# Tables of powers times B and powers times C made on GpSimd one batch ahead, in buffers of their own

## The chip, the cores and the metric

The kernel runs on one core of a Trainium2 chip. The metric is the time of one execution on the device, in microseconds (us). The core has five engines that run side by side, each with its own queue of instructions that it executes in order: TensorE (PE, matrix products), VectorE (DVE), ScalarE (ACT), GpSimd (POOL) and SyncE (SP), which here issues most of the DMAs. An instruction waits for semaphores of the others, and whatever is queued behind it on its engine waits too.

## The reference, cut to what matters

One layer of an encoder over 1024 tokens of width 1024: a norm, a wide product z = hn @ w_in, four mixers on slices of z (a gated recurrence, a neighbourhood attention, a state space mixer, a pooling), and a gated merge. The change concerns the state space mixer, which is for 32 groups of 16 channels, 64 complex states and two directions:

```python
for d in range(2):
    ...
    bu_r = jnp.einsum('bsgc,gpc->bsgp', ug, bbar_r)
    bu_i = jnp.einsum('bsgc,gpc->bsgp', ug, bbar_i)
    _, _, sr, si = lax.associative_scan(_complex_combine, (a_r, a_i, bu_r, bu_i), axis=1, reverse=(d == 1))
    yd = (jnp.einsum('bsgp,gcp->bsgc', sr, c_re[d]) - jnp.einsum('bsgp,gcp->bsgc', si, c_im[d]))
    y = y + yd.reshape(bsz, s, w)
yg = jax.nn.gelu(y)
return yg * jax.nn.sigmoid(yg @ glu_w + glu_b)
```

## The kernel before, in words

Every large product is made of three products of split operands (a high and a low part, `wh` and `wl`, `hnH` and `hnL`; lines 94 to 96, `mm3`). The program runs through stages: the norm, the attention, the state space mixer, its gated unit (`glu`), the recurrence (`lru`), the pooling, the merge. Products of z that no stage needs at once are the filler. They come from a generator, `z_gen`: each of its steps is 24 products of 128x512 into PSUM (`ps_z`, `ps_t`), with an eviction (ACT, and for the branch gates one DVE product, `bgt`), and every second step also splits a block of weights into `wh` (ACT) and `wl` (DVE).

`drive` mixes a stage with the filler. The stage is a generator that yields pairs (estimated PE time, estimated DVE time); a scale multiplies the DVE part, 1.25 for the state space stage, 1.35 for the gated unit and 0.95 for the recurrence. As long as the summed PE time is behind the DVE time, one filler step (5.2 of PE) is emitted:

```python
pe = dve = 0.0
for p, v in main:
    pe, dve = pe + p, dve + v * scale
    while filler is not None and pe < dve:
        c = next(filler, None)
        ...
        pe, dve = pe + c[0], dve + c[1]
```

What the filler has left after the recurrence is emitted then. A scheduler of the framework afterwards sets each engine's order from this order of emission and from its own simulated times. The queues of the order below are what it made.

The state space stage (`s5`) first makes parameters (`s5_params`): powers of the state matrix (`Ag`, `Aq`, `Pm`) and the inputs `Bb` and `Ct`. It then works through four batches (`s5_batch`) of 8 groups. In a batch, `Gf` is the table of powers times B (two tiles of 128x1024) and `Q` that of powers times C (two of 128x1280), each made of three elementwise operations with a temporary (`gt`, `qt`). PE transposes Gf into `Gt` (line 99) and multiplies Bb with Q (line 975), from which the short convolution `M` comes by way of DRAM. `E` holds further powers, made on DVE, and lies in the buffers of Gf. Then two halves follow: PE makes V from U and Gt (line 1022), DVE turns V into `vr` and `vi`, scans them (lines 1046 and 1048) and turns the results `xs` into `Xr` and `Xi`; PE adds U times M (line 1068), Xr times Q and Xi times Q (line 1070); ACT copies the sum to `Y`. Eight DMAs write Y of a batch to `ydr` in DRAM (line 1075). The gated unit reads it back as `gy` (line 1085), makes the gelu (`gt`, `yg`, split into `ygH` and `ygL`), and multiplies with the split weights `gw`.

Of the kernel before, what the change touches and what calls it, by code (L numbers as in the profile page):

```python
# [9 lines left out]
F32 = mybir.dt.float32  # L10
# [3 lines left out]
ALU = mybir.AluOpType  # L14
# [17 lines left out]
class Kern:  # L32
# [23 lines left out]
    def tt(self, out, a, b, op):  # L56
        self.nc.vector.tensor_tensor(out, a, b, op)
# [847 lines left out]
    def s5(self):  # L905
        self.ydr = self.dp.tile([W, 8, 128], F32, name="ydr")
        self.kd = [self.dp.tile([16, 2, 4, 240], F32, name=f"kd{k}") for k in range(4)]
        with self.tc.tile_pool(name="sp", bufs=1, reuse_waits="tile") as sp:
            with self.tc.tile_pool(name="sq", bufs=1, reuse_waits="tile") as sq:
                self.s5_params(sp, sq)  # L910
            yield 1.0, 22.0
            with self.tc.tile_pool(name="sb", bufs=1, reuse_waits="tile") as sb:
                for ct in range(4):
                    yield from self.s5_batch(sb, ct)

    def s5_batch(self, sb, ct):
        nc = self.nc
        g8 = slice(ct * 8, ct * 8 + 8)

        def bcg(tab, n):  # L920
            return tab[:, :, g8].rearrange("p n g -> p g n").unsqueeze(3).broadcast_to([128, 8, n, 16])

        def bcc(m, n):
            return m.unsqueeze(2).broadcast_to([128, 8, n, 16])
        Bv = [bcc(b[:, g8, 0:16], 8) for b in self.Bb]
        Cv = [bcc(c.rearrange("p (g c) -> p g c", c=16)[:, g8, :], 10) for c in self.Ct]

        U = sb.tile([128, 8, 128], F32, tag="U", name="U")
        for t in range(8):
# [1 line left out]
                              self.ud[ct * 128:ct * 128 + 128, t, :].rearrange("(g c) j -> c g j", c=16))  # L931

        Gt = []
        gs = [128, 8, 8, 16]
        Gf = [sb.tile(gs, F32, tag=f"Gf{k}", name=f"Gf{k}") for k in range(2)]
        gt = sb.tile(gs, F32, tag="tmpA", name="gt")
        self.mul(Gf[0], bcg(self.Ag[0], 8), Bv[0])
        self.mul(gt, bcg(self.Ag[1], 8), Bv[1])
        self.sub(Gf[0], Gf[0], gt)
        gt = sb.tile(gs, F32, tag="tmpA", name="gt")  # L940
        self.mul(Gf[1], bcg(self.Ag[0], 8), Bv[1])
        self.mul(gt, bcg(self.Ag[1], 8), Bv[0])
        self.add(Gf[1], Gf[1], gt)
        yield 0.0, 7.0
        for k in range(2):
            o = sb.tile([128, 8, 128], F32, tag=f"Gt{k}", name=f"Gt{k}")
            for h in range(2):
# [4 lines left out]
                self.copy_a(o[:, h * 4:h * 4 + 4, :], pt.rearrange("p (g n) -> p g n", g=4))  # L952
            Gt.append(o)
        yield 2.0, 0.0

        qs = [128, 8, 10, 16]
        Q = [sb.tile(qs, F32, tag=f"Q{k}", name=f"Q{k}") for k in range(2)]
        qt = sb.tile(qs, F32, tag="tmpA", name="qt")
        self.mul(Q[0], bcg(self.Aq[0], 10), Cv[0])
        self.mul(qt, bcg(self.Aq[1], 10), Cv[1])  # L960
        self.sub(Q[0], Q[0], qt)
        qt = sb.tile(qs, F32, tag="tmpA", name="qt")
        self.mul(Q[1], bcg(self.Aq[2], 10), Cv[0])
        self.mul(qt, bcg(self.Aq[0], 10), Cv[1])
        self.sub(Q[1], Q[1], qt)
        yield 0.0, 8.4

        pk = [self.ps("s").rearrange("p (a b) -> p a b", a=4) for _ in range(2)]
        for gi in range(2):
            for q in range(4):  # L970
                g = gi * 4 + q
                for half, lo in ((0, 0), (1, 2)):
                    p = slice(64 * half, 64 * half + 64)
                    for k in range(2):
                        nc.tensor.matmul(
                            pk[half][32 * q:32 * q + 32, gi, :],
                            self.Bb[k][p, ct * 8 + g, :],
                            Q[k][p, g, lo:lo + 8, :].rearrange("p t c -> p (t c)"),
                            start=(k == 0), stop=(k == 1),
# [21 lines left out]
        for m in range(7):  # L1001
            n = 1 << m
            b = [128, 8, n]
# [12 lines left out]
        for h in range(2):  # L1016
# [10 lines left out]
            vr, vi, t = (sb.tile(hv, F32, tag=n, name=n) for n in ("vr", "vi", "vt"))  # L1027
# [3 lines left out]
            t = sb.tile(hv, F32, tag="vt", name="vt")  # L1031
# [11 lines left out]
            for k, vv in ((0, vr), (1, vi)):  # L1043
                x = sb.tile(hv, F32, tag=f"xs{k}", name=f"xs{k}")
# [10 lines left out]
            t = sb.tile(hv, F32, tag="vt", name="vt")  # L1055
# [3 lines left out]
            t = sb.tile(hv, F32, tag="vt", name="vt")  # L1059
# [5 lines left out]
            for g in range(4):  # L1065
                c = slice(g * 128, g * 128 + 128)
                a = h * 4 + g
                nc.tensor.matmul(py[:, c], M[:, a, :], U[:, a, :], start=True, stop=False)
                for k in range(2):
                    nc.tensor.matmul(py[:, c], Q[k][:, a, 1:9, :].rearrange("p t c -> p (t c)"), X[k][:, c],  # L1070
                                     start=False, stop=(k == 1))
# [338 lines left out]
```

## Time and profile before

| | |
|---|---|
| median of 3 runs | 1368.45 us (1367.85 to 1368.73) |
| profiled execution | 1368.02 us, its span 1366.2 us |
| PE busy | 1346.5 us (99%) |
| DVE busy | 918.9 us (67%) |
| ACT busy | 565.0 us (41%) |
| POOL busy | 20.9 us (2%) |

The profile is of one execution. The span is the time from its first to its last recorded instruction. Busy time is the time in which an engine executes; the rest of the span it waits. In a row, a group of instructions is named by its line in the program, its engine, its operation and its tiles as out<-in. The state space stage's batches lie between about 408 and 702 us of the span.

### The profile page before, as it was taken

What the parts mean: (1) busy time and instruction counts of PE and PEld (TensorE: products, weight loads), DVE (VectorE), ACT (ScalarE), POOL (GpSimd) and SP (SyncE); (2) the same over time, 40 slices, a digit from 0 to 9 for tenths busy, and PEclk for the clock granted to TensorE, in tenths of its full rate; (3) what the DMA queues carried; (4) which work ended last, traced back from release to release, by engine and by line L of the source; (5) the groups of instructions that cost most, each with busy time, mean ns of one, the idle gap of its engine ahead of it and who ended that gap; (6) DMA issues with size and microseconds to landing.
All of it is one profiled execution on the core that took longest, in us unless ns stands there. A gap on an engine that the chain in (4) does not pass through costs nothing.

```text
span 1366.2 us, 19163 instructions
## 1 busy us (share of the span) xinstructions
PE 1346.5 (99%) x7354; PEld 1142.2 (84%) x7354; DVE 918.9 (67%) x1664; ACT 565.0 (41%) x881; POOL 20.9 (2%) x81
## 2 busy tenths in 40 slices
PE   7999999999999999999999999999999999999997
PEld 6999998888888888788888888888888888888885
DVE  6551676455289797979758367356465676896886
ACT  6552676587532221212134545526322211154552
POOL 2200000000000000000000000000000000000000
PEclk9999999999999999999999999999999999999998
DMA  9452134433344233323344142232824657433326
GB/s 326 130 146 65 54 83 121 131 97 121 86 120 120 81 100 121 94 96 103 118 160 162 57 153 97 82 139 89 298 99 175 240 170 268 164 108 124 124 93 216
DMA packets 141054, 181.98 MB, mean 133 GB/s; under 512 B 29200, under 2 KB 100888, under 8 KB 140962
## 3 DMA queue, kind: packets, MB, share of 16 engines
q1 hardware_dynamic: 140610, 180.72, 40.6%
q8 instruction: 58, 0.95, 0.3%
q14 instruction: 34, 0.28, 0.1%
q0 software_dynamic: 352, 0.03, 0.0%
HBM read 127.05 MB, written 54.03 MB: 133 GB/s over the span
## 4 chain that ended last, share of the span: by engine, by line
PE 92%; DVE 5%; DMA 1%; issue 1%; ACT 0%; SPq 0%; DVEq 0%
PE ps_z L94 15%; PE ps_z L95 15%; PE ps_z L96 15%; PE ps_t L96 4%; PE ps_t L95 4%; PE ps_t L94 4%; PE ps_t L99 3%; PE ps_o L94 3%; PE ps_o L96 3%; PE ps_o L95 3%; PE ps_s L94 3%; PE ps_s L96 3%; PE ps_s L95 3%; PE ps_o L580 2%; PE ps_s L545 2%; PE ps_z L1326 1%
## 5 line engine op out<-in xcount | busy, mean ns | idle before, releaser
L94 PE MATMUL ps_z<-hnH,wh 128*128 128x512 f32 x744 | 293.2, 394 | 2.0 <-DVE bgt L60 2.0
L95 PE MATMUL ps_z<-hnL,wh 128*128 128x512 f32 x744 | 292.0, 392 | 0.0
L96 PE MATMUL ps_z<-hnH,wl 128*128 128x512 f32 x744 | 291.8, 392 | 0.0
L94 PEld LDWEIGHTS ps_z<-hnH,wh 128*128 128x128 f32 x744 | 139.8, 188 | 30.8 <-DVE bgt L60 2.4
L96 PEld LDWEIGHTS ps_z<-hnH,wl 128*128 128x128 f32 x744 | 139.8, 188 | 28.5 <-issue 0.4
L95 PEld LDWEIGHTS ps_z<-hnL,wh 128*128 128x128 f32 x744 | 139.8, 188 | 27.8 <-issue 0.4
L66 DVE TENSOR_TENSOR wl<-wr,wh 128x1024 fp32r<-128x1024 f32 x72 | 88.0, 1222 | 101.2 <-ACT wh L82 101.1
L82 ACT ACTIVATE wh<-wr 128x1024 fp32r<-128x1024 f32 x72 | 76.1, 1059 | 148.6 <-PE ps_z L95 81.1
L94 PE MATMUL ps_z<-wh,hnH 128*128 128x256 f32 x384 | 108.3, 285 | 0.5 <-ACT zqk L82 0.5
L96 PE MATMUL ps_z<-wh,hnL 128*128 128x256 f32 x384 | 108.5, 287 | 0.0
L95 PE MATMUL ps_z<-wl,hnH 128*128 128x256 f32 x384 | 108.1, 283 | 0.0
L95 PE MATMUL ps_t<-hnL,wh 128*128 128x512 f32 x216 | 84.2, 390 | 0.0
L94 PE MATMUL ps_t<-hnH,wh 128*128 128x512 f32 x216 | 84.1, 389 | 0.0
L96 PE MATMUL ps_t<-hnH,wl 128*128 128x512 f32 x216 | 84.0, 389 | 0.0
L94 PEld LDWEIGHTS ps_z<-wh,hnH 128*128 128x128 f32 x384 | 73.2, 191 | 1.2 <-ACT zqk L82 1.2
L95 PEld LDWEIGHTS ps_z<-wl,hnH 128*128 128x128 f32 x384 | 73.5, 192 | 0.0
L96 PEld LDWEIGHTS ps_z<-wh,hnL 128*128 128x128 f32 x384 | 72.9, 192 | 0.0
L551 DVE CUSTOM_DVE_ANT_0 sc<-ps_s,bias 128x384 f32<-128x384 f32 x64 | 34.2, 555 | 27.2 <-PE ps_s L545 14.6
L94 PE MATMUL ps_o<-my,wh 128*128 128x512 f32 x128 | 49.9, 390 | 0.4 <-DVE pm L69 0.4
L78 ACT ACTIVATE gz<-ps_z 128x512 f32<-128x512 f32 x45 | 26.7, 593 | 56.9 <-issue 35.1
L94 PE MATMUL ps_s<-my,wh 128*128 128x512 f32 x128 | 49.8, 389 | 0.0
L96 PE MATMUL ps_s<-my,wl 128*128 128x512 f32 x128 | 49.8, 389 | 0.0
(417 smaller groups left out, 2732.2 us busy)
## 6 DMA issues: line engine op xcount, KB each, us to landing
wr<-in_w_in_dram SPq DMA_DIRECT2D x32, 1024.0 KB, 5.4
gd<-gz SPq DMA_DIRECT2D x32, 512.0 KB, 2.8
mgt<-gd SPq DMA_DIRECT2D x32, 512.0 KB, 4.0
sg<-bgt SPq DMA_DIRECT2D x16, 512.0 KB, 3.1
my<-yd SPq DMA_DIRECT2D x16, 512.0 KB, 4.2
mbr<-in_w_branch_dram SPq DMA_DIRECT2D x8, 1024.0 KB, 6.1
bias<-E SPq DMA_DIRECT2D x128, 48.0 KB, 2.0
xt<-in_x_dram SPq DMA_DIRECT2D x8, 512.0 KB, 10.0
```

The lines of the kernel that those rows point to most:

```text
L66: self.nc.vector.tensor_tensor(out, a, b, ALU.subtract)
L78: self.nc.scalar.activation(out, a, f, **kw)
L82: return self.nc.scalar.activation(out, a, AF.Copy)
L94: mm(ps, aH, bH, start=(k == 0), stop=False)
L95: mm(ps, aH, bL, start=False, stop=False)
L96: mm(ps, aL, bH, start=False, stop=(k == n - 1))
L99: self.nc.tensor.transpose(ps, src, self.ident[:k, :k])
L545: nc.tensor.matmul(pss[h], q[h][:, qs], km[h][(slice(0, 128),) + ks], start=(p == 0), stop=(p == 1))
L551: nc.vector.tensor_tensor_reduce(sc, pss[h], bias[g][h][:, VIDX[j], :], 1.0, -3e38, ALU.add, ALU.max, mx)
L580: m = self.nc.tensor.matmul(po[64 * h:64 * h + 64, j * 128:j * 128 + 128], vb[:, g + c, j, h * 64:h * 64 + 64], PT[h][:, c * 128:c * 128 + ...
L1326: mm(acc[g], aH[:, k, c], bH[:, k, :], start=begin, stop=False, skip_group_check=True)
```

## The change

The twelve elementwise operations of a batch that make Gf and Q leave `s5_batch`, with their two yields, (0.0, 7.0) and (0.0, 8.4). A new function, `s5_tables`, makes the same two tables with `tensor_tensor` on GpSimd. `s5` calls it for batch 0 before the loop and then for batch ct + 1 ahead of batch ct. Gf gets buffers of its own (tag `Gg`), so that E alone has the tags `Gf`; Q has two buffers for each of its tiles; both temporaries share one tag, `tmpA`.

```diff
             with self.tc.tile_pool(name="sb", bufs=1, reuse_waits="tile") as sb:
+                tab = self.s5_tables(sb, 0)
                 for ct in range(4):
-                    yield from self.s5_batch(sb, ct)
+                    nxt = self.s5_tables(sb, ct + 1) if ct < 3 else None
+                    yield from self.s5_batch(sb, ct, *tab)
+                    tab = nxt
...
+        gs, qs = [128, 8, 8, 16], [128, 8, 10, 16]
+        Gf = [sb.tile(gs, F32, tag=f"Gg{k}", name=f"Gf{k}") for k in range(2)]
+        Q = [sb.tile(qs, F32, tag=f"Q{k}", name=f"Q{k}", bufs=2) for k in range(2)]
+        tt = self.nc.gpsimd.tensor_tensor
+        for out, shape, a, x, b, y, op in (
+                (Gf[0], gs, bcg(self.Ag[0], 8), Bv[0], bcg(self.Ag[1], 8), Bv[1], ALU.subtract),
+                (Gf[1], gs, bcg(self.Ag[0], 8), Bv[1], bcg(self.Ag[1], 8), Bv[0], ALU.add),
+                (Q[0], qs, bcg(self.Aq[0], 10), Cv[0], bcg(self.Aq[1], 10), Cv[1], ALU.subtract),
+                (Q[1], qs, bcg(self.Aq[2], 10), Cv[0], bcg(self.Aq[0], 10), Cv[1], ALU.subtract)):
+            t = sb.tile(shape, F32, tag="tmpA", name="gt")
+            tt(out, a, x, ALU.mult)
+            tt(t, b, y, ALU.mult)
+            tt(out, out, t, op)
+        return Gf, Q
...
-        Gf = [sb.tile(gs, F32, tag=f"Gf{k}", name=f"Gf{k}") for k in range(2)]
-        gt = sb.tile(gs, F32, tag="tmpA", name="gt")
-        self.mul(Gf[0], bcg(self.Ag[0], 8), Bv[0])
-        self.mul(gt, bcg(self.Ag[1], 8), Bv[1])
-        self.sub(Gf[0], Gf[0], gt)
...
-        yield 0.0, 7.0
...
-        Q = [sb.tile(qs, F32, tag=f"Q{k}", name=f"Q{k}") for k in range(2)]
-        qt = sb.tile(qs, F32, tag="tmpA", name="qt")
-        self.mul(Q[0], bcg(self.Aq[0], 10), Cv[0])
-        self.mul(qt, bcg(self.Aq[1], 10), Cv[1])
-        self.sub(Q[0], Q[0], qt)
...
-        yield 0.0, 8.4
```

On PE, the end of the last batch stands so before: its last products with M, Xr and Xi, and behind them the first of 90 filler products (`hnH`, `hnL`).

```order
L1068 MATMUL ps_s<-U,M 128x128
L1070 MATMUL ps_s<-Xr,Q_6739 128x128
L1070 MATMUL ps_s<-Xi,Q_6740 128x128
L94 MATMUL ps_z<-hnH,wh 128x512
L95 MATMUL ps_z<-hnL,wh 128x512
L96 MATMUL ps_z<-hnH,wl 128x512
L94 MATMUL ps_z<-hnH,wh 128x512
```

And so now, from the end of the seventh half on (line 1020 is V, 1066 and 1068 the products with M, Xr and Xi):

```order
L1068 MATMUL ps_s<-Xr,Q_5750 128x128
L1068 MATMUL ps_s<-Xi,Q_5751 128x128
L1020 MATMUL ps_s<-U,Gt_6248 128x128 x4
L1066 MATMUL ps_s<-U,M 128x128
L1068 MATMUL ps_s<-Xr,Q_5750 128x128
L1068 MATMUL ps_s<-Xi,Q_5751 128x128
...
L1066 MATMUL ps_s<-U,M 128x128
L1068 MATMUL ps_s<-Xr,Q_5750 128x128
L1068 MATMUL ps_s<-Xi,Q_5751 128x128
L94 MATMUL ps_s<-ygH_6757,wh 128x512
L94 MATMUL ps_o<-ygH_6757,wh 128x512
```

The filler products between the last half's V and its X products, and those between the last X product and the first product of the gated unit (`ygH`), have moved behind the stage.

On POOL, one small memset of the parameters and then those of the recurrence stand in a row before:

```order
L880 MEMSET dq 8x128
L620 MEMSET up 128x2
L621 MEMSET up 128x1
L620 MEMSET up 128x2
L621 MEMSET up 128x1
```

Now the tables stand between them, 48 operations, of which these are the first eleven (`Gf_4784` and `Gf_4785` are Gf of batch 0, `Q_4786` and `Q_4787` its Q, `Q_4806` and `Q_4807` the Q of batch 1):

```order
L880 MEMSET dq 8x128
L940 TENSOR_TENSOR Gf_4784<-Ag_4508,Bb_4476 128x1024
L941 TENSOR_TENSOR gt<-Ag_4509,Bb_4477 128x1024
L940 TENSOR_TENSOR Gf_4785<-Ag_4508,Bb_4477 128x1024
L940 TENSOR_TENSOR Q_4786<-Aq_4488,Ct_4571 128x1280
L940 TENSOR_TENSOR Q_4787<-Aq_4490,Ct_4571 128x1280
L940 TENSOR_TENSOR Q_4806<-Aq_4488,Ct_4571 128x1280
L940 TENSOR_TENSOR Q_4807<-Aq_4490,Ct_4571 128x1280
L942 TENSOR_TENSOR Gf_4784<-Gf_4784,gt 128x1024
L941 TENSOR_TENSOR gt<-Ag_4509,Bb_4476 128x1024
L942 TENSOR_TENSOR Gf_4785<-Gf_4785,gt 128x1024
L941 TENSOR_TENSOR gt<-Aq_4489,Ct_4572 128x1280
```

The scheduler has put four first products of Q ahead of the operations that finish batch 0's Gf.

## Rows read from the trace of the kernel before

**Rows 1.** The page's engines: busy us (share of the span), instructions.

```profile
PE 1346.5 (99%) x7354; PEld 1142.2 (84%) x7354; DVE 918.9 (67%) x1664; ACT 565.0 (41%) x881; POOL 20.9 (2%) x81
```

**Rows 2.** Waits: engine, line, waited for: us in total, times, longest us.

```profile
PE ps_z L94 <- DVE bgt L60: 2.0, 2, 1.6
```

**Rows 3.** Windows, the stage's batches (columns in the first row).

```profile
core 0: us, PE busy (x) PEld busy (x) DVE busy (x) ACT busy (x) POOL busy (x), PEclk, DMA share, GB/s
408.00:702.00 294.00, 291.99 (x1694) 244.55 (x1693) 248.61 (x463) 65.61 (x104) 0.00 (x0) 1.00 0.33 102
```

**Rows 4.** Timeline of PE: start us, us, engine line op, tiles, count.

```profile
420.89 1.03 PE L99 MATMUL ps_t<-ident,Gf 128*128 128x128 f32 x8
...
700.60 0.39 PE L1070 MATMUL ps_s<-Xi,Q 128*128 128x128 f32 x2
...
720.14 0.39 PE L95 MATMUL ps_t<-hnL,wh 128*128 128x512 f32 x1
...
721.05 0.39 PE L96 MATMUL ps_t<-hnH,wl 128*128 128x512 f32 x1
```

**Rows 5.** Groups on DVE, 408 to 702 us: busy us, mean ns | idle before.

```profile
L66 DVE TENSOR_TENSOR wl<-wr,wh 128x1024 fp32r<-128x1024 f32 x21 | 25.6, 1220 | 5.1 <-ACT wh L82 5.0
L60 DVE TENSOR_TENSOR bgt<-bgt,ps_z 128x512 f32<-128x512 f32 x24 | 16.4, 682 | 2.9 <-ACT bgt L78 2.8
...
L60 DVE TENSOR_TENSOR Q<-Aq,Ct 128x1280 f32<-128x1280 f32 x8 | 11.6, 1486 | 0.2 <-PE ps_s L1070 0.2
L60 DVE TENSOR_TENSOR vt<-ps_s,E 128x512 f32<-128x512 f32 x16 | 11.0, 690 | 14.6 <-PE ps_s L1022 14.0
...
L60 DVE TENSOR_TENSOR Gf<-Ag,Bb 128x1024 f32<-128x1024 f32 x8 | 9.8, 1219 | 0.0
...
L60 DVE TENSOR_TENSOR vr<-ps_s,E 128x512 f32<-128x512 f32 x8 | 5.5, 687 | 10.6 <-PE ps_s L1070 10.6
```

**Rows 6.** Timeline of DVE: the first table operation, and the last half.

```profile
408.57 1.22 DVE L60 TENSOR_TENSOR Gf<-Ag,Bb 128x1024 f32<-128x1024 f32 x1
...
682.82 0.69 DVE L60 TENSOR_TENSOR vt<-ps_s,E 128x512 f32<-128x512 f32 x1 [5.46 <-PE ps_s L1022]
...
691.81 1.22 DVE L66 TENSOR_TENSOR wl<-wr,wh 128x1024 fp32r<-128x1024 f32 x1
692.97 0.06 DVE L1050 MEMSET xs<- 64x4 f32 x1
...
694.42 0.69 DVE L66 TENSOR_TENSOR Xr<-Xr,vt 128x512 f32<-128x512 f32 x1
...
695.86 0.69 DVE L63 TENSOR_TENSOR Xi<-Xi,vt 128x512 f32<-128x512 f32 x1
```

**Rows 7.** Timeline of SP's queue: issues of the DMAs behind the last batch.

```profile
701.64 3.65 SPq L1075 DMA_DIRECT2D ydr<-Y  x8
705.39 0.85 SPq L1085 DMA_DIRECT2D gy<-ydr  x2
```

**Rows 8.** Timeline of ACT: from the last Y to the third ygH.

```profile
701.02 0.60 ACT L82 ACTIVATE Y<-ps_s 128x512 f32<-128x512 f32 x1 [2.33 <-PE ps_s L1070]
...
709.07 1.06 ACT L78 ACTIVATE gt<-gy 128x1024 f32<-128x1024 f32 x1 [2.59 <-DMA gy<-ydr]
...
715.54 1.99 ACT L83 ACTIVATE ygH<-yg 128x1024 fp32r<-128x1024 f32 x2
...
725.29 1.05 ACT L83 ACTIVATE ygH<-yg 128x1024 fp32r<-128x1024 f32 x1
```

**Rows 9.** Groups on POOL: busy us, mean ns | idle before.

```profile
L407 POOL MEMSET bias<- 128x1152 f32 x4 | 4.1, 1064 | 9.3 <-PE ps_z L95 6.7 <-PE ps_t L99 2.7
...
masks.py:199 POOL TENSOR_SCALAR_AFFINE_SELECT ident<-ident 128x128 f32<-128x128 f32 x1 | 0.3, 290 | 0.0
...
L1395 POOL MEMSET const-float32-1.0<- 128x1 f32 x1 | 0.1, 99 | 0.0
```

More of the change, by code (lines that the diff above doesn't have):

```diff
@@ L912, in s5, with s5_tables @@
             with self.tc.tile_pool(name="sb", bufs=1, reuse_waits="tile") as sb:
+                tab = self.s5_tables(sb, 0)
                 for ct in range(4):
-                    yield from self.s5_batch(sb, ct)
-    def s5_batch(self, sb, ct):
-        nc = self.nc
+                    nxt = self.s5_tables(sb, ct + 1) if ct < 3 else None
+                    yield from self.s5_batch(sb, ct, *tab)
+                    tab = nxt
+    def s5_tables(self, sb, ct):
         g8 = slice(ct * 8, ct * 8 + 8)
@@ L926, in s5_batch @@
         Cv = [bcc(c.rearrange("p (g c) -> p g c", c=16)[:, g8, :], 10) for c in self.Ct]
+        gs, qs = [128, 8, 8, 16], [128, 8, 10, 16]
[12 more added lines that the diff above has]
+        return Gf, Q
+    def s5_batch(self, sb, ct, Gf, Q):
+        nc = self.nc
+        g8 = slice(ct * 8, ct * 8 + 8)
         U = sb.tile([128, 8, 128], F32, tag="U", name="U")
@@ L933, in s5_batch @@
         Gt = []
-        gs = [128, 8, 8, 16]
-        Gf = [sb.tile(gs, F32, tag=f"Gf{k}", name=f"Gf{k}") for k in range(2)]
-        gt = sb.tile(gs, F32, tag="tmpA", name="gt")
-        self.mul(Gf[0], bcg(self.Ag[0], 8), Bv[0])
-        self.mul(gt, bcg(self.Ag[1], 8), Bv[1])
-        self.sub(Gf[0], Gf[0], gt)
[L940 to L943, printed above, removed]
-        yield 0.0, 7.0
         for k in range(2):
@@ L954, in s5_batch @@
         yield 2.0, 0.0
-        qs = [128, 8, 10, 16]
-        Q = [sb.tile(qs, F32, tag=f"Q{k}", name=f"Q{k}") for k in range(2)]
-        qt = sb.tile(qs, F32, tag="tmpA", name="qt")
-        self.mul(Q[0], bcg(self.Aq[0], 10), Cv[0])
-        self.mul(qt, bcg(self.Aq[1], 10), Cv[1])
-        self.sub(Q[0], Q[0], qt)
[L962 to L965, printed above, removed]
-        yield 0.0, 8.4
         pk = [self.ps("s").rearrange("p (a b) -> p a b", a=4) for _ in range(2)]
```

## The prediction

> **What bounds the kernel now.** I read the page's engine table first. TensorE (PE) is busy 1346.5 of 1366.2 us, so it stands idle for 19.7 us in all; VectorE (DVE) is busy 67%, and GpSimd (POOL) did 20.9 us of work [rows 1]. The waits of PE come next: of its filler products only one group waits for DVE, twice, 2.0 us together [rows 2]. The stretches then show the state space stage: from 408 to 702 us PE is busy 291.99 of 294.00, DVE 248.61, and POOL not at all [rows 3]. So PE is the bound, and in this stage too. Time can only be won where PE stands still, at most 2.0 us here. It is lost wherever PE runs out of products while it waits for a chain of other engines. The profiled execution took 1368.02 us, 0.4 below the median of 1368.45; my sum starts from 1368.0 and I expect the same distance to a median.
>
> What keeps PE full is the filler, the z products of 128x512. They start 0.2275 us apart: 721.05 less 720.14, over four [rows 4]. The groups of DVE by shape show what the twelve removed instructions of a batch cost: 1.22 us each for the 24 of 128x1024 and 1.49 us for the 24 of 128x1280 [rows 5].
>
> **The change part by part.**
>
> *Removed from DVE*: 24 x 1.22 + 24 x 1.49 = 65.0 us. PE waited for DVE 2.0 us only, so I book -2.0 and nothing more: the rest of those 65 us lay beside filler products.
>
> *Removed with it: the estimates.* Each batch drops two yields of 7.0 and 8.4. At the stage's scale of 1.25 that is 4 x 15.4 x 1.25 = 77 us of DVE time against which the driver emits filler steps of 5.2: 15 steps, or 360 products, fewer. The order agrees: between the first transposes of Gf and the last Xi product 990 z products stand before, and 631 now. These 359 x 0.2275 = 81.5 us are not saved; they stand after the stage, and PE does them later. What matters is whether 631 are enough to cover the stage's chains. There are four places.
>
> 1. Last half of the last batch. The order puts no z product between its V products and its X products now (63 before; 42 to 59 in the other seven halves, against 59 to 84). The timeline of DVE shows that chain: V is read from 682.82, and Xr is done at 694.42 + 0.69 = 695.11 [rows 6]. Within it stands one filler split (wl, 691.81 to 692.97, 1.16), which goes with the filler. PE waits 12.29 - 1.16 = 11.1 us for Xr and 1.4 more for Xi (695.86 + 0.69): +12.5 us. Before, filler hid all of it.
>
> 2. Tail. PE's last X product ends at 700.99 [rows 4]. Y is copied, written by eight DMAs and read back as gy (SP: 701.64, 705.39) [rows 7], and goes through the gelu on ScalarE and DVE, until the first ygH is done at about 716.5 [rows 8]. Before, 90 z products stand in front of the first product of ygH (20.5 us, more than the chain's 15.5). Now there are none, and PE is in order: +15.5. It could be 14.2, since ygH stood behind two filler copies (wh).
>
> 3. The gated unit behind it. Its products read four ygH tiles; the third is done at 725.29 + 1.05 = 726.34 [rows 8]. PE would have used up the 24 products of the first two tiles at 716.5 + 24 x 0.2275 = 722.0: +4.3. Then four evictions of about 1 us each (a 128x512 copy takes 0.60 [rows 8], and the semaphores on both sides) have no filler beside them: +4. I take +8.3, bounds 3 and 9.
>
> 4. The seven other halves. Chain with filler's DVE work in it: 11.1 + 1.16 + 0.68 for one bgt [rows 5] = 12.9. The cover left is 53, 43, 59, 43, 48, 47 and 42 products of 0.2275, and the shortfalls add up to 14.5. Some of PE's own products fall in it, so I take +11, bounds 0 and 15.
>
> *Added: 48 tensor_tensors on POOL, and no DMA.* No row shows one there. The nearest rows are a memset of 1152 elements, 1064 ns, against 99 ns for one element (0.84 ns an element for a write), and an affine_select of 128 elements, 290 ns (1.48 ns an element beyond the 99 ns, one read and one write) [rows 9]. A second read at the difference, 0.65, makes 2.13 ns: 2.28 us for 1024 elements, 2.83 for 1280, and 24 x 2.28 + 24 x 2.83 = 122.6 us. Bounds: 0.84 ns an element (48 x about 1.1 = 51 us) and twice the middle (245 us). The stage lasts some 236 us now (294 - 81.5 + 12.5 + 11), so at the middle POOL is half busy, and from batch 1 on it is far ahead. Only batch 0 is close. The removed work began at 408.57 [rows 6]; the order puts eight operations up to the end of Gf0 and ten up to Gf1 (four Q products stand between): 408.6 + 4 x 2.28 + 4 x 2.83 = 429.0 for Gf0. PE's first transposes stood at 420.89 [rows 4], and 44 more z products stand ahead of them now: 430.9. They just meet. I book 0, bounds 0 and, at twice the price, +18.5 (20.4 more, less the 1.9 to spare).
>
> *Added: POOL beside DVE.* Before, POOL is idle in the whole stage [rows 3], so no row shows an instruction of POOL that reads SBUF beside one of DVE that reads two SBUF operands. Lower end 0: they don't disturb each other. Upper end: each instruction of POOL keeps such DVE work waiting for its whole length. Only DVE's work with one operand in PSUM stays free: bgt 16.4 us, vt 11.0, and vr and vi another 11.0 at the same 0.69 [rows 5], 38.4 in all. Then DVE is delayed by 122.6 - 38.4 = 84 us. DVE has idle time to absorb some of it: 248.6 - 65.0 - 8 x 1.22 leaves 174 us busy of 236 (the order has 13 splits, wl, in the stage instead of 21). A delay counts where it falls in a chain on which PE has no cover left: eight halves of 12.4 us are 99 of 236 us, or 42%, and 42% of 84 is 35. I take +35, a little under the middle of 0 and 84.
>
> The Trainium skill has a rule for this pair (SBUF — State Buffer, "Who interferes with whom"): a VectorE instruction with two SBUF inputs contends with a GpSimd instruction that reads SBUF, and the later one is blocked until the other has finished. By that rule the term is above zero, without it the sum would stop at 1413; no run here has shown it so far.
>
> **Sum.** -2.0 + 12.5 + 15.5 + 8.3 + 11 = +45.3 from the missing cover, +35 from POOL beside DVE: 1368.0 + 80.3 = 1448 us.
>
> **Rivals.**
>
> *No contention: 1413 us* (1404 to 1420 by the bounds of places 2 to 4). For it: nothing in the trace says that POOL and DVE disturb each other. The same sum without the 35. It would show as DVE durations and gaps unchanged beside a busy POOL.
>
> *POOL is late: about 1480 us.* If an operation costs twice the middle, POOL has 245 us of work in a stage of 236 and becomes its bound: +18.5 at the start, and the DVE delays reach the upper end, 245 - 38 = 207 us, of which at least 42%, or 87, count. Even half of that beside the 45 and 18.5 gives 1368 + 45 + 18.5 + 43 = 1475, and all of it 1519. For it: the tables' operands are broadcast views with an innermost run of 16, which no POOL row shows. Against it: the rows of 9 would have to mislead by a factor of two.
>
> *Not slower: 1366 us.* One mechanism: the chains close by themselves. With 65 us less in its queue DVE comes to V, scans and X products earlier, and if ScalarE and SP also ran the tail while PE still had earlier products, PE would never stand still; only the -2.0 is left. It decides at the last half: PE would need 12.5 us of products between V and X. Against it: the order has none there, none in the tail, PE runs in order, and gy stands behind the last batch's ydr writes on SP, so no earlier gelu fills the gap. The first DVE operation of that chain is released by PE itself (idle 5.46 us before it [rows 6]), so less DVE work doesn't shorten it.
>
> *Little filler is missed: 1393 us.* If places 3 and 4 come out at their lower bounds and the place 1 chain is 3 us shorter, without contention: the sum is 1366 + 9.5 + 14.2 + 3 = 1393. For it: places 3 and 4 rest on counts of products, not on a wait that a row shows.
>
> **How the numbers follow.** Contention with the cover missing 0.47 (1448; its own range 1420 to 1490); no contention 0.34 (1413); POOL late 0.09 (1475 and up); little filler missed 0.05; not slower 0.05. The range leaves out the last two and the part of POOL late above 1490: 1405 to 1490. A measurement of this kernel tells no difference below about 0.2%, 2.7 us. Faster by more than that needs more than the 2.0 us that there are to win: 0.02. Within 0.2%: 0.03. Slower: 0.95.
>
> **What would show it.** The cover: PE idle some 15 us between the last Xi product and the first ygH product, some 10 us waiting for Xr in the last half, and about 65 us idle in all without contention. The contention: DVE's two-operand instructions with longer durations or gaps while POOL is busy, the one-operand ones (bgt) unchanged, and the stage's last Xi product near 675 us; without it near 640. POOL's price: its 48 rows near 2.3 and 2.8 us. POOL's lateness: waits of PE for Gf or Q by POOL, which I expect under 3 us. I am wrong if PE is idle under 30 us in all, or if the loss lies in waits for Gf and Q.

## The result, and the profile after

The changed kernel takes 1493.6 us (median of four runs, 1492.06 to 1494.3) against 1368.15: 1.0915 of the time before, interval 1.0899 to 1.0932. The prediction had the side right and missed the size: 1448, with a range that ended at 1490.

The engine table of the changed kernel, in the columns of [rows 1]:

```profile
span 1492.5 us, 19174 instructions
...
PE 1378.1 (92%) x7354; PEld 1161.7 (78%) x7354; DVE 943.8 (63%) x1616; ACT 566.0 (38%) x881; POOL 141.7 (9%) x129
```

Three numbers follow by subtraction. PE stands idle for 1492.5 - 1378.1 = 114.4 us, 94.7 more than before. Its 7354 instructions, as many as before, were busy 31.6 us longer. Together that is the whole loss of 126.3 us of span. And DVE should be busy 858.9 us: the durations of the 48 operations that left it add up to 65.0 us, but consecutive records on DVE overlap by about 0.1 us, so that without them its busy time before is 60.0 us less. It was 943.8, so 84.9 us went into making its own instructions longer.

The waits of PE name the places (in total, times, longest):

```profile
PE ps_z L94 <- DVE bgt L60: 26.9, 3, 17.7
PE ps_z L96 <- DVE wl L66: 21.3, 2, 20.3
PE ps_s L94 <- ACT ygH L83: 15.2, 2, 14.9
PE ps_s L1068 <- DVE Xr L66: 13.9, 4, 9.0
PE ps_z L94 <- ACT wh L82: 4.9, 4, 2.2
```

The third and fourth lines are the places without cover that the prediction named. The first two, 48 us, are not: filler products wait for the filler's own DVE work (2.0 us in [rows 2]). PE's timeline shows the largest, with the releaser in brackets:

```profile
438.48 0.39 PE L95 MATMUL ps_z<-hnL,wh 128*128 128x512 f32 x1
459.19 0.79 PE L96 MATMUL ps_z<-hnH,wl 128*128 128x512 f32 x1 [20.32 <-DVE wl L66]
459.79 0.63 PE L94 MATMUL ps_z<-hnH,wh 128*128 128x512 f32 x1
460.21 0.63 PE L95 MATMUL ps_z<-hnL,wh 128*128 128x512 f32 x1
```

The split wl for which PE waits needs wh from ACT, which was long there: ACT began it at 438.23. What holds it up is DVE's queue. Its timeline from the first operation of the E table on, with POOL's beside it:

```profile
411.14 1.89 DVE L60 TENSOR_TENSOR E<-E,Pm 128x8 f32<-128x8 f32 x1
412.94 0.16 DVE L60 TENSOR_TENSOR Et<-E,Pm 128x8 f32<-128x8 f32 x1
413.02 2.49 DVE L60 TENSOR_TENSOR E<-E,Pm 128x8 f32<-128x8 f32 x1
...
451.84 2.38 DVE L66 TENSOR_TENSOR E<-E,Et 128x128 f32<-128x128 f32 x1
...
457.92 1.22 DVE L66 TENSOR_TENSOR wl<-wr,wh 128x1024 fp32r<-128x1024 f32 x1
...
461.69 0.69 DVE L63 TENSOR_TENSOR E<-E,Et 128x512 f32<-128x512 f32 x1
```

```profile
438.23 1.06 ACT L82 ACTIVATE wh<-wr 128x1024 fp32r<-128x1024 f32 x1 [1.65 <-PE ps_z L95]
```

```profile
410.94 2.06 POOL L940 TENSOR_TENSOR Gf<-Ag,Bb 128x1024 f32<-128x1024 f32 x1 [4.63 <-DVE Pm L66]
412.96 9.97 POOL L940 TENSOR_TENSOR Q<-Aq,Ct 128x1280 f32<-128x1280 f32 x4
...
449.58 2.08 POOL L941 TENSOR_TENSOR gt<-Ag,Bb 128x1024 f32<-128x1024 f32 x1
451.73 2.34 POOL L942 TENSOR_TENSOR Gf<-Gf,gt 128x1024 f32<-128x1024 f32 x1
```

An operation on 8 elements a partition takes 0.16 us undisturbed and 1.89 or 2.49 when it meets a POOL instruction; the first ends at 413.03, as POOL's does at 413.00. E of the first batch stretches from 411.14 to 462.38, 51 us, where its 42 operations add up to 12.9 us in the kernel before, and wl stands in it behind the 128x256 operations. DVE counts as busy all the time, so that its busy share tells nothing of this; the durations do. The operations with one operand in PSUM stay as they were in [rows 5]:

```profile
L60 DVE TENSOR_TENSOR bgt<-bgt,ps_z 128x512 f32<-128x512 f32 x20 | 13.6, 682 | 14.4 <-ACT bgt L78 14.3
...
L60 DVE TENSOR_TENSOR vt<-ps_s,E 128x512 f32<-128x512 f32 x16 | 11.0, 690 | 9.1 <-PE ps_s L1020 8.8
```

The stretches give the lower clock (us, PE, PEld, DVE, ACT, POOL busy, PEclk, DMA share, GB/s); the rows from 700 on are the last half and the tail:

```profile
400.00:440.00 40.00, 38.87 (x180) 32.01 (x178) 39.69 (x68) 10.66 (x16) 32.88 (x15) 1.00 0.27 80
440.00:464.00 24.00, 4.81 (x11) 3.47 (x11) 23.55 (x26) 0.00 (x0) 13.68 (x6) 0.53 0.00 0
...
540.00:560.00 20.00, 2.34 (x7) 1.57 (x6) 19.76 (x21) 0.60 (x1) 12.93 (x6) 0.60 0.26 72
...
700.00:720.00 20.00, 7.97 (x32) 6.93 (x32) 12.70 (x21) 0.60 (x1) 0.00 (x0) 0.52 0.00 0
720.00:740.00 20.00, 4.71 (x22) 4.23 (x22) 6.62 (x8) 6.20 (x8) 0.00 (x0) 0.59 0.60 187
```

Where PE had been idle for long, the granted clock is near half, which is the lower of its two levels, 1.2 instead of 2.4 GHz. After the 20.32 us of waiting, filler products start 0.42 us apart (459.79, 460.21) instead of 0.2275. Of the whole execution the mean clock is 0.960, against 0.997.

At the end of the stage things go as the prediction had them, only later (the last Xi product ends at 725.74, not near 675):

```profile
707.05 2.08 PE L1020 MATMUL ps_s<-U,Gt 128*128 128x128 f32 x8 [0.73 <-ACT Y L82]
710.60 0.77 PE L1066 MATMUL ps_s<-U,M 128*128 128x128 f32 x2 [1.47 <-DVE vi L60]
720.37 0.79 PE L1068 MATMUL ps_s<-Xr,Q 128*128 128x128 f32 x2 [9.00 <-DVE Xr L66]
721.82 0.80 PE L1068 MATMUL ps_s<-Xi,Q 128*128 128x128 f32 x2 [0.66 <-DVE Xi L63]
...
725.35 0.39 PE L1068 MATMUL ps_s<-Xi,Q 128*128 128x128 f32 x2
...
740.66 0.79 PE L94 MATMUL ps_s<-ygH,wh 128*128 128x512 f32 x1 [14.92 <-ACT ygH L83]
```

Three of POOL's groups by shape (busy us, mean ns):

```profile
L942 POOL TENSOR_TENSOR Q<-Q,gt 128x1280 f32<-128x1280 f32 x8 | 24.4, 3050 | 0.4
...
L940 POOL TENSOR_TENSOR Q<-Aq,Ct 128x1280 f32<-128x1280 f32 x8 | 19.9, 2519 | 28.5 <-PE ps_s L1068 28.5
L942 POOL TENSOR_TENSOR Gf<-Gf,gt 128x1024 f32<-128x1024 f32 x8 | 19.4, 2421 | 0.6
```

### The profile page after: what moved, and what is told of

It reads as the page before. It is cut to its first block, busy times and chain, and to the rows that moved or that the text cites. A ratio compares the mean times of both kernels' runs of the same rounds, so it can differ in the third digit from the quotient of the medians.

```text
span 1492.5 us, 19174 instructions
## 1 busy us (share of the span) xinstructions
PE 1378.1 (92%) x7354; PEld 1161.7 (78%) x7354; DVE 943.8 (63%) x1616; ACT 566.0 (38%) x881; POOL 141.7 (9%) x129
## 4 chain that ended last, share of the span: by engine, by line
PE 76%; DVE 16%; DMA 3%; issue 2%; ACT 1%; SPq 1%; DVEq 0%; ACTq 0%
PE ps_z L94 11%; PE ps_z L95 11%; PE ps_z L96 11%; PE ps_t L94 4%; PE ps_t L95 4%; PE ps_t L96 4%; PE ps_t L99 3%; PE ps_o L94 2%; PE ps_o L96 2%; PE ps_o L95 2%; PE ps_s L95 2%; PE ps_s L96 2%; PE ps_s L94 2%; DVE Et L60 2%; DVE E L60 2%
## 5 line engine op out<-in xcount | busy, mean ns | idle before, releaser
L94 PE MATMUL ps_z<-hnH,wh 128*128 128x512 f32 x672 | 268.5, 400 | 31.0 <-DVE bgt L60 26.9
L96 PE MATMUL ps_z<-hnH,wl 128*128 128x512 f32 x672 | 267.5, 398 | 21.3 <-DVE wl L66 21.3
L95 PE MATMUL ps_z<-hnL,wh 128*128 128x512 f32 x672 | 267.8, 399 | 0.0
L96 PEld LDWEIGHTS ps_z<-hnH,wl 128*128 128x128 f32 x672 | 128.9, 192 | 48.7 <-DVE wl L66 22.1
L95 PEld LDWEIGHTS ps_z<-hnL,wh 128*128 128x128 f32 x672 | 128.8, 192 | 26.4 <-issue 0.6
L94 PE MATMUL ps_t<-hnH,wh 128*128 128x512 f32 x288 | 112.6, 391 | 0.7 <-ACT Gt L82 0.7
L95 PE MATMUL ps_t<-hnL,wh 128*128 128x512 f32 x288 | 112.4, 390 | 0.0
L96 PE MATMUL ps_t<-hnH,wl 128*128 128x512 f32 x288 | 112.3, 390 | 0.0
L94 PEld LDWEIGHTS ps_t<-hnH,wh 128*128 128x128 f32 x288 | 54.2, 188 | 12.0 <-ACT Gt L82 0.9
L96 PEld LDWEIGHTS ps_t<-hnH,wl 128*128 128x128 f32 x288 | 54.1, 188 | 11.6 <-issue 0.4
L95 PEld LDWEIGHTS ps_t<-hnL,wh 128*128 128x128 f32 x288 | 54.3, 188 | 11.3
```

The lines of the kernel that those rows point to most:

```text
L94: mm(ps, aH, bH, start=(k == 0), stop=False)
L95: mm(ps, aH, bL, start=False, stop=False)
L96: mm(ps, aL, bH, start=False, stop=(k == n - 1))
```

## The experiments

Theory 1: two losses that add up, the filler that is no longer emitted, and DVE's instructions waiting for POOL's; the lower clock follows from both. Rivals: all of it is the one or the other, or the new order of the queues. All are compared by PE idle (span less busy) and PE busy, beside 19.7 and 1346.5 before. "DVE lost" is its busy time less the 858.9 us.

**e1: the two yields put back.**

```diff
         Gt = []
+        yield 0.0, 7.0
...
         yield 2.0, 0.0
+        yield 0.0, 8.4
```

> The changed kernel, with the two yields (0.0, 7.0) and (0.0, 8.4) put back into the batch, so that the driver emits the 15 filler steps against them again; the tables stay on GpSimd. Theory 1 (missing filler, 45 us, and contention, each with its share, the lower clock following from PE's idle time): the cover terms go (last half, tail and gated unit covered again: -36 us and more), while VectorE's instructions still wait for GpSimd's and the E chain of the first batches still holds up the filler's own wl and bgt in VectorE's queue: 1385 to 1440 us, VectorE busy again some 90 us above its sum without contention. Rival (all is missing filler, the stretched E chain only shows because PE has nothing else): 1366 to 1375 us. Rival (all is contention): 1480 us or more.

1438.3 us, 1.0513 (1.0496 to 1.0531).

```profile
span 1435.9 us, 19179 instructions
...
PE 1359.1 (95%) x7354; PEld 1150.5 (80%) x7354; DVE 946.7 (66%) x1616; ACT 564.6 (39%) x881; POOL 140.8 (10%) x129
```

Its waits of PE:

```profile
PE ps_z L94 <- DVE bgt L60: 32.4, 3, 17.4
PE ps_z L96 <- DVE wl L66: 20.6, 1, 20.6
PE ps_s L1070 <- DVE Xr L66: 5.2, 1, 5.2
```

At the top edge of what theory 1 said, and both rivals are out. PE idle 76.8 (+57.1 over before), busy +12.6. The wait for ygH is gone, so the tail was missing filler. The waits for wl and bgt, 53 us, stay: more filler doesn't help when the filler's own work stands in the stretched queue. Three of them, of 20.6, 17.4 and 11.9 us, end while DVE works on the E of the first, second and third batch.

**e2: the kernel before, with only the yields dropped.**

```diff
-        yield 0.0, 7.0
...
-        yield 0.0, 8.4
```

> The kernel before, with only the two yields dropped: the tables stay on VectorE, GpSimd does nothing in the stage, and the filler of the changed kernel is missing. Theory 1: no contention, so VectorE's durations are those of before; the cover is missing as in the changed kernel (+45 us) and the 65 us of tables now stand in chains with less filler beside them, so PE idles for part of them as well, 20 to 65 us: 1430 to 1480 us, PE idle 85 to 130 us, and PE's busy time above 1346.5 by 10 to 30 us through the lower clock. Rival (the missing filler alone costs little and contention makes the loss): under 1400 us.

1456.2 us, 1.0644 (1.0622 to 1.0665), as theory 1 had it. PE idle 90.6, busy 1362.7. So two lines of estimates, with the same instructions in another order, cost 88 us by themselves as long as DVE makes the tables. That part of the loss needs no GpSimd.

**e3: POOL writes, but doesn't read.**

```diff
-            tt(out, a, x, ALU.mult)
-            tt(t, b, y, ALU.mult)
-            tt(out, out, t, op)
+            for o in (out, t, out):
+                for r in range(2):
+                    self.nc.gpsimd.memset(o, 0.0)
```

> The changed kernel, but each GpSimd tensor_tensor is replaced by two memsets of its output (no operand is read; the tables are zero, so the products with them are left out in value, not in time). GpSimd is as busy, about 1.0 us a memset, some 100 us in all, but reads nothing. Theory 1 (VectorE's instructions with two SBUF operands wait for GpSimd instructions that read SBUF): VectorE's durations as before (0.18 us for the smallest E operations), PE idle about 65 us, 1410 to 1435 us with a little lower clock. Rival (any work of GpSimd beside VectorE slows it): 1480 us or more, the E operations again at 2 us. Rival (it is the order of the queues, not contention): 1480 or more, with VectorE's durations short.

The tables are zeros here, so their values are left out of the output.

1425.5 us, 1.042 (1.0399 to 1.044).

```profile
span 1422.3 us, 19220 instructions
...
PE 1360.5 (96%) x7354; PEld 1149.3 (81%) x7354; DVE 858.7 (60%) x1616; ACT 565.5 (40%) x881; POOL 119.0 (8%) x177
```

DVE is busy 858.7 us, what it should be without contention, beside 98.1 us more of POOL than before; memsets run beside the whole E of the first batch, which takes 13.2 us. The E operations on 64 elements, by shape, first here and then in the changed kernel:

```profile
L60 DVE TENSOR_TENSOR E<-E,Pm 128x64 f32<-128x64 f32 x8 | 1.4, 218 | 0.0
```

```profile
L60 DVE TENSOR_TENSOR E<-E,Pm 128x64 f32<-128x64 f32 x8 | 8.9, 1147 | 0.0
```

POOL's writes alone disturb nothing, and the order of the queues isn't it; what delays the E operations is a POOL instruction that reads. (e3 changes the instruction along with its reads, and no run keeps the one and drops the other. Its length is not the cause: the memsets take about 1.0 us, and the shorter products of e4 still delay.) PE idle 61.8 (+42.1), busy 1360.5 (+14.0): that is the missing cover without contention. With e1's +57.1 and +12.6 the two make +99.2 idle and +26.6 busy, against +94.7 and +31.6 measured in the changed kernel: they add up nearly. How nearly is counted from e7.

**e4: each POOL operation in four.**

```diff
-            tt(out, a, x, ALU.mult)
...
+            for o, p, q, f in ((out, a, x, ALU.mult), (t, b, y, ALU.mult), (out, out, t, op)):
+                for g in range(0, 8, 2):
+                    tt(o[:, g:g + 2], p[:, g:g + 2], q[:, g:g + 2], f)
```

> The changed kernel, but each GpSimd tensor_tensor is issued as four, over two groups each, about 0.6 us instead of 2.4, the same elements in all. Theory 1a (a VectorE instruction waits for one whole GpSimd instruction, however short it is itself): the small E operations wait 0.6 us at most, the E chain of the first batch (46 us, 411 to 457) shrinks to about 20 to 28, PE's idle time beside it goes, and the time falls to 1425 to 1460 us. Theory 1b (the two share a bandwidth: VectorE loses time in proportion to GpSimd's bytes): the E chain and the time stay where they are, 1485 to 1510 us.

1478.2 us, 1.0804 (1.0783 to 1.0826): between the two theories, and each was half wrong.

```profile
L60 DVE TENSOR_TENSOR E<-E,Pm 128x64 f32<-128x64 f32 x8 | 5.3, 701 | 0.0
```

The longest E product fell from 3.03 to 1.22 us, so an operation does wait for one POOL instruction, and less for a shorter one. But nearly every E operation now meets one (38 of the first 42 are delayed, against 18 in the changed kernel), and the first E chain still takes from 411.70 to 443.41, 32 us. DVE lost 66.3 us instead of 84.9. POOL pays too: a quarter takes 0.78 to 1.02 us on average, not 0.6, 164.0 us in all instead of 120.8, and PE now waits for Gf and Q here and there (2.9 us each).

**e5: e1, with one operand of each E operation in PSUM.**

```diff
+        pP = self.ps("o")[:, 0:112].rearrange("p (k m g) -> p k m g", k=2, m=7)
+        pE = self.ps("o").rearrange("p (g n) -> p g n", g=8)
+        for k in range(2):
+            self.copy_a(pP[:, k], self.Pm[k][:, :, g8])
...
-            P = [self.Pm[k][:, m, g8].unsqueeze(2).broadcast_to(b) for k in range(2)]
-            t0 = sb.tile([128, 8, 64], F32, tag="Et", name="Et")[:, :, 0:n]
+            P = [pP[:, k, m, :].unsqueeze(2).broadcast_to(b) for k in range(2)]
+            t0 = pE[:, :, 0:n]
...
```

> As e1 (tables on GpSimd, the two yields back), and each operation of the E chain has one operand in PSUM: the powers Pm of a batch are copied there by ScalarE (two copies of 56 elements), and the temporaries (Et) lie there. The elements and their order are those of e1. Theory (a VectorE instruction waits for GpSimd when both its operands are in SBUF; in the E chains these waits hold up the filler's own wl and bgt in VectorE's queue, and so PE, for 53 of e1's 57 us of extra idle time): the E operations of the first batch are short again (0.2 to 0.7 us, the chain some 13 us instead of 46), the two waits of 20.6 and 17.4 us go, PE idles 25 to 40 us in all, 1373 to 1395 us. Rival (contention moves to the scans and X products, where GpSimd's work now falls): 1415 to 1440 us.

1394.7 us, 1.019 (1.0173 to 1.0207): 43.6 us less than e1, at the upper end of the theory's range. DVE by shape, then the waits of PE:

```profile
L66 DVE TENSOR_TENSOR wl<-wr,wh 128x1024 fp32r<-128x1024 f32 x24 | 38.7, 1613 | 15.9 <-ACT wh L82 15.8
...
L1050 DVE TENSOR_TENSOR_SCAN xs<-dk,vr 64x511 f32<-64x511 f32 x8 | 12.8, 1606 | 0.0
...
L60 DVE TENSOR_TENSOR E<-E,ps_o 128x64 f32<-128x64 f32 x8 | 1.7, 214 | 0.0
```

```profile
PE ps_z L94 <- DVE bgt L60: 9.0, 3, 4.5
PE ps_s L1074 <- DVE Xr L66: 6.3, 1, 6.3
```

The E operations run beside POOL at their undisturbed 0.21 us; the first chain takes 13.2 us (413.19 to 426.43) and the wait of 20.6 us is gone, and the longest for bgt is 4.5 us instead of 17.4. What still has two SBUF operands, the scans (1.20 in e3) and the splits (1.22 in [rows 5]), meets POOL instead. PE idle 36.2, busy +10.0, DVE lost 35.8 us.

**e6: the same in the changed kernel without the yields.**

```diff
+        pP = self.ps("o")[:, 0:112].rearrange("p (k m g) -> p k m g", k=2, m=7)
+        pE = self.ps("o").rearrange("p (g n) -> p g n", g=8)
...
+            P = [pP[:, k, m, :].unsqueeze(2).broadcast_to(b) for k in range(2)]
+            t0 = pE[:, :, 0:n]
...
```

> The changed kernel without the yields, with the E chain's operands in PSUM as in e5. If the two losses add up (missing cover 56 us with its lower clock, contention 70 us of which the E chains hold most), this comes to 1425 to 1455 us: e3's 1425 plus what the scans and X products still lose. Rival (with less filler, contention in V and X costs as much as in E): 1465 us or more.

1450.9 us, 1.0603 (1.0582 to 1.0625): in the range of the sum. Taking the E chains out of POOL's way gains 42.7 us here and 43.6 in e5, with the filler missing and with it there.

**e7: both causes gone** (memsets in place of the tables again, whose values are left out).

```diff
+        yield 0.0, 7.0
...
+        yield 0.0, 8.4
...
+            for o in (out, t, out):
+                for r in range(2):
+                    self.nc.gpsimd.memset(o, 0.0)
```

> As e3 (memsets in place of GpSimd's products, so the tables' values are left out), with the yields back. Both causes are gone: 1364 to 1373 us, PE idle 18 to 25 us. A remainder of more than 5 us would be a third cause, such as the new order of the queues. That the removed 65 us of VectorE's work are worth something by themselves would show as 1366 us or less.

1371.7 us, 1.003 (1.002 to 1.004).

```profile
span 1368.3 us, 19224 instructions
...
PE 1348.7 (99%) x7354; PEld 1143.2 (84%) x7354; DVE 859.6 (63%) x1616; ACT 565.2 (41%) x881; POOL 119.0 (9%) x177
```

PE idle 19.6, as before. There is no third cause of the size of these two. A remainder of 3.4 us is clear of noise; in the profiled execution, 2.1 us longer than before, PE is busy 2.2 us more. Why stays open. The four spans with and without each cause, in us:

| | yields there | yields gone |
|---|---|---|
| POOL writes only | 1368.3 (e7) | 1422.3 (e3) |
| POOL reads, too | 1435.9 (e1) | 1492.5 (changed kernel) |

The missing yields alone cost 54.0 us, POOL's reads alone 67.6, together 121.6; both at once cost 124.2. And 59 us less DVE work gained nothing: no version that was run beats the kernel before, where PE has 19.7 us of idle time, 2.0 of them waiting for DVE in filler.

## Why the prediction was wrong, step by step

- **PE is the bound, and the 65 us off DVE are worth at most 2.0.** Right, and shown by e7.
- **The missing filler, +45.3.** The total was nearly right as idle time: +42.1 in e3. Its parts there, by PE's idle time: the last half 11.1 us (12.5 predicted; in the changed kernel 9.00 + 0.66 + 1.47), the tail 15.1 (15.5), the gated unit 3.5 (8.3), the stage up to the last half 6.7 more than before (9.0, its 11 less the 2.0). Another 5.4 us came behind the gated unit, where the sum had nothing. So the two long waits were understood, and that the total came within 3.2 us is in part luck. The four evictions in the gated unit, put at 1 us each, which no row shows, cost no wait: PE waited there for ygH (1.0) and for split weights (2.4). e1 brings the last half, the tail and the gated unit to nothing.
- **POOL's price, 122.6 us.** 120.8 measured; by group 2.18 to 2.42 us for 1024 elements and 2.52 to 3.05 for 1280, around the predicted 2.28 and 2.83. The interpolation between a memset and an affine_select held, for the sum of the two kinds: products of broadcast views lie below it, differences and sums of whole tiles above.
- **POOL in time for batch 0.** Right: no wait of PE for Gf or Q stands in the changed kernel's list; Gf0 was done at 425.3 (429.0 predicted) and PE's transposes began at 429.4 (430.9). So "POOL is late" is false, though its 1475 to 1519 is the only case that held the measured time.
- **POOL beside DVE, +35.** This is a step that failed. Its upper end, a delay of 84 us, is what happened (84.9). The 42% was wrong: it let a delay count only in the chains between V and X, and of those e1 shows one wait, 5.2 us for Xr. The table of E, 42 operations per batch of 0.16 to 0.69 us each, does not appear in that term. Its operations took 51.0, 30.5, 25.0 and 12.9 us in the four batches (the sums of their durations; before, 12.9 in each, and in the last batch POOL has no table left to make): 67.7 of the 84.9 us. Each of them can lose a whole POOL instruction, and the order puts the first E just where POOL makes most of the tables of batches 0 and 1, 18 instructions beside it, and 18 of the 42 were delayed. Behind them in DVE's queue stand the filler's wl and bgt, so even a PE with enough filler stops: the three waits of e1 that end there are 49.8 of its 57.1 us. Had all of the 84 us counted, the sum would have come to 1497, which the range, ending at 1490, left out.
- **The lower clock.** This is the other step that failed: the sum had no term for it. PE's instructions were busy 14.0 us longer with the missing cover (e3), 12.6 with contention (e1) and 31.6 with both; e7, with a mean clock of 0.999, has 2.2 of that, so that up to 29.4 us go with the lower clock. From the predicted 1448.3 to the profiled 1494.3 it is 46.0 us: 22.1 for contention's 57.1 in place of 35 and 31.6 for PE's longer busy time, less 3.2 for the cover and 4.5 because with both at once PE idles less than in the two apart.
- **The rivals.** No contention, 1413: e3 is that case and took 1425, where PE's busy time is 14.0 us longer. (The bounds of places 2 to 4 give 1396 to 1418 for it, not 1404 to 1420.) Little filler missed: false, by e3's +42.1. Not slower: false.

The rule of the Trainium skill (SBUF — State Buffer, "Who interferes with whom") that the prediction names agrees with all that was run. VectorE's instructions with one operand in PSUM were not disturbed (bgt 682 ns as in [rows 5], vt 690, E in e5 214). Memsets of POOL disturbed nothing (e3). And in the changed kernel 37 VectorE instructions with two SBUF operands began inside a tensor_tensor of POOL, over 0.2 us before its end; each of the 37 ended only when that one had ended.

## What to carry to other kernels

Moving work to an idle engine is free only if neither engine blocks the other. On this chip count the VectorE instructions with two SBUF operands that run beside GpSimd's reading ones, not their microseconds, and ask what stands behind them in VectorE's queue. And where estimates steer how much filler is emitted, an operation taken off an engine takes its cover along: keep the estimate, or look for the chain that it covered. One operand in PSUM took the short operations out of GpSimd's way here (43 us gained in e5 and in e6). Add to PE's waits what the lower clock behind the long ones costs, by rows at that level.

## What the runs showed of the hardware

- A POOL tensor_tensor of f32 with both operands in SBUF takes 2.0 to 2.3 ns an element (2.04 us for 1024 with broadcast views, 2.34 to 2.40 for the difference of two whole tiles), against 1.22 us on DVE for 1024. Issued in quarters it takes 0.78 to 1.02 us each on average, beside DVE.
- A DVE operation of 0.16 us with two SBUF operands takes up to 2.5 us beside it, and the profile counts the wait as busy.
- Waits of PE of 9 us and more all ended at the lower clock, and PE worked on at it: after 20.32 us, filler products started 0.42 us apart until 463.6, and 0.23 us apart from 465.6 on.
